# The RWKV scan batches start on the keys alone, and the gate's product moves behind receptances and values

## The chip, the cores and the metric

The kernel runs on one core of a Trainium2 chip. The time is the device time of one execution in microseconds (us). The engines are TensorE (PE in the rows; PEld is its loading of weights), VectorE (DVE), ScalarE (ACT), GpSimd (POOL) and SyncE (SP), which only issues DMA transfers. Every engine works through its own list of instructions, and semaphores tie the lists together.

## The reference, cut to what matters

Two layers act on 256 tokens of width 2048 (128 context tokens, 128 latent ones). The mixer of a layer has three parts side by side, fed by one input projection and merged by one output projection: attention with a sink (12 heads), a Hyena long convolution (512 channels), and the bidirectional RWKV-7 time mixing (768 channels, 12 heads of 64). The change touches the last of these:

```
rkv = short_conv(u_rkv)                      # three taps along the tokens
r, k, v = split(rkv, 3)
decay, a = functions of low-rank products    # w_dn, a_dn
g  = sigmoid(g_dn) @ g_up                    # the gate, low rank 256
kk = k * k_k;  kk = kk / max(norm(kk over a head), 1e-12)
...                                          # the scan, in both directions:
S  = S * decay - (S kk) (kk a) + v k_dir     # one 64x64 state per head
y  = S r
```

The scan of the latent tokens starts from a cached state. Behind the mixer stands an MLP with squared ReLU (hidden width 8192), and every sub-layer sits between two norms with modulation.

## The kernel before, in words

**Products.** The big matrix products run on PE in three passes of reduced fp32 each, so one product is three rows of the profile. `ws` holds the weights still and streams 256 token columns (L508, L511, L512); `as_` holds the activations still and streams up to 512 weight columns (L530, L533, L534). A weight tile comes in by SyncE (`wr`, L231), ScalarE rounds it (`wh`, L232) and VectorE forms the rest (`wl`, L233). Tiles `wr` have four buffers, `wh` and `wl` three each, in a ring: the cast of a tile waits until PE has used the tile three before it. The results of products go to `mm`, of which there are two buffers in PSUM, and each buffer is read by a short convolution (`conv`: one ScalarE instruction L543 and two VectorE instructions L544, L545 for each block of 128 channels) or added up (`acc`). Products `ada` (L387), which make modulation vectors for later, are strewn between the others and also fill gaps.

**Side work.** Everything else that the mixer does is written as generators in a class `Side`: a queue of chains, each of which is stepped on at a rate that depends on the columns of the product just issued (`run`; the rates are the options `sr`, `sq`, `sh`, `so`, `ra`). What a chain yields is a delay before its next step. Their small matmuls stand behind the last product issued, in program order, by a dependency without a semaphore (`beside`); they write to `sm`, with three buffers in PSUM. A scheduler then fixes the order of each engine's list.

**The order in `mixer`.** Low-rank products and the keys k of batch 0, their convolution, the product of the gate and `rwkv_gate`, receptances r and values v of batch 0 (`rkv(0, "rv")`); then the chain of RWKV work joins the side queue. Products of attention's q, k, v follow (512 columns), and attention and Hyena join the queue. Then come k, r, v of batch 1, the three Hyena inputs (256 columns again, the last one feeds tiles `hu0`), and the output projection `w_out` in phases.

**The chain of RWKV work.** It is batch 0 (channel blocks 0 to 2), its output, batch 1 (blocks 3 to 5), its output. A batch (`rwkv_batch`, L1093) waits until r, k and v of its three blocks are there; loads small matrices (`rwkv_up`); loads and transposes the starting states (`rwkv_state`, `rs`); takes the norms of the keys (`rwkv_kk`); runs three scan blocks (`rwkv_stage1`, which goes from the low-rank product L837 through decays and scans on VectorE and ScalarE to the transposes L897, the score products L921 into `sm`, the masked copies L924 and L925, L939 and L942, and the transposes L950); inverts triangular matrices (`rwkv_invert`: reads `rX` by DMA L973, 30 pairs L981 and L982 on VectorE, copies L987 and L988 to `rXo`, writes `rdout` by DMA L994); and finishes (`rwkv_stage2`: reads `rXT` by two DMAs L1002, the products L1021 with `rXT`, L1019 and what follows).

## Time and profile before

| | |
|---|---|
| median of 3 runs | 2888.81 us (2887.84 to 2892.58) |
| the profiled execution | 2894.91 us, span 2893.1 us |
| mean granted clock of TensorE | 0.983 |
| busy: PE / DVE / ACT / POOL | 97% / 57% / 43% / 6% of the span |
| mixer of the first layer | about 160 to 720 us of the span |
| mixer of the second layer | about 1550 to 2125 us of the span |

The page counts an engine as busy while an instruction of its datapath runs. In a timeline row the first number is the start in us from the start of the span, the second the duration, xN the instructions merged into the row, and the brackets at the end give the idle time before it and what ended that. Matmuls overlap in the pipeline, so the distance between starts, not the duration, is what a product costs. PEclk is the granted clock of TensorE as a share of its full speed.

### The profile page before, as it was taken

Reading aid. Unit: us, or ns where it says so; the run is one execution under the profiler, and the core shown is the slowest. Engines: PE = TensorE matmul, PEld = TensorE weight load, DVE = VectorE, ACT = ScalarE, POOL = GpSimd, SP = SyncE. Lnnn points to the kernel's source line nnn. Section 1 sums busy time; section 2 is a strip of 40 time slices with the busy share of each in tenths; the row PEclk is TensorE's granted clock in tenths of the full one; section 3 lists DMA queues with packets and bytes.
Section 4 is the critical chain, followed back from the end, with each engine's and each line's share of the span. In section 5 each row is a group of like instructions: output and inputs, shape, how many; then the busy total and the mean of one; then the engine's idle time right before and its main releaser. Section 6 shows DMA issues by size and latency. Waiting matters only on the chain. (4 is left out here: it accounts for less than half of the span.)

```text
span 2893.1 us, 47892 instructions
## 1 busy us (share of the span) xinstructions
PE 2810.1 (97%) x19163; PEld 2306.6 (80%) x19163; DVE 1646.9 (57%) x2635; ACT 1232.4 (43%) x1878; POOL 179.4 (6%) x368
## 2 busy tenths in 40 slices
PE   6899999999999999999998999999989999999998
PEld 3586888766797897897876979877669989899896
DVE  1356766777544454444455577677675545555555
ACT  2254445434544343343345454453354444444343
POOL 0012101202000000000000111011010000000000
PEclk8999999999999999999999999999899999999999
DMA  9985675478888787887876746534686666666674
GB/s 333 333 300 201 223 231 161 152 261 285 311 268 268 261 270 256 272 274 262 288 279 210 210 149 193 168 111 142 200 297 184 184 186 185 189 189 183 190 241 150
DMA packets 326185, 654.56 MB, mean 226 GB/s; under 512 B 48709, under 2 KB 86158, under 8 KB 325835
## 3 DMA queue, kind: packets, MB, share of 16 engines
q1 hardware_dynamic: 311456, 610.88, 65.3%
q0 software_dynamic: 12928, 36.98, 3.9%
q10 hardware_dynamic: 1579, 3.64, 0.3%
q8 instruction: 150, 2.46, 0.3%
q14 instruction: 72, 0.59, 0.1%
HBM read 632.21 MB, written 19.20 MB: 225 GB/s over the span
## 5 line engine op out<-in xcount | busy, mean ns | idle before, releaser
L233 DVE TENSOR_TENSOR wl<-wr,wh 128x1024 fp32r<-128x1024 f32 (+2 forms) x792 | 929.0, 1175 | 921.1 <-ACT wh L232 909.6
L232 ACT CAST wh<-wr 128x1024 fp32r<-128x1024 f32 (+2 forms) x792 | 798.7, 1010 | 1175.5 <-PE mm L511 522.6
L508 PE MATMUL mm<-acth,wh 128*128 128x256 f32 (+1 forms) x3200 | 921.2, 288 | 6.5 <-ACT acth L489 4.6
L511 PE MATMUL mm<-actl,wh 128*128 128x256 f32 (+1 forms) x3200 | 904.7, 283 | 0.0
L512 PE MATMUL mm<-acth,wl 128*128 128x256 f32 (+1 forms) x3200 | 902.9, 282 | 1.9 <-DVE wl L233 1.9
L508 PEld LDWEIGHTS mm<-acth,wh 128*128 128x128 f32 (+1 forms) x3200 | 601.8, 188 | 59.2 <-issue 32.1
L512 PEld LDWEIGHTS mm<-acth,wl 128*128 128x128 f32 (+1 forms) x3200 | 602.8, 188 | 7.3 <-DVE wl L233 4.3
L511 PEld LDWEIGHTS mm<-actl,wh 128*128 128x128 f32 (+1 forms) x3200 | 600.9, 188 | 4.5 <-issue 3.3
L530 PE MATMUL mm<-wh,fh 128*128 128x512 f32 x1024 | 404.9, 395 | 0.0
L533 PE MATMUL mm<-wl,fh 128*128 128x512 f32 x1024 | 403.3, 394 | 1.0 <-DVE wl L233 0.9
L534 PE MATMUL mm<-wh,fl 128*128 128x512 f32 x1024 | 401.6, 392 | 0.0
L530 PEld LDWEIGHTS mm<-wh,fh 128*128 128x128 f32 x1024 | 192.2, 188 | 56.6 <-issue 8.4
L533 PEld LDWEIGHTS mm<-wl,fh 128*128 128x128 f32 x1024 | 192.2, 188 | 44.9 <-DVE wl L233 2.7
L534 PEld LDWEIGHTS mm<-wh,fl 128*128 128x128 f32 x1024 | 192.0, 187 | 45.2
L387 PE MATMUL ada<-wa,cs 128*32 128x512 f32 x1280 | 193.3, 609 | 8.4 <-DMA wa<-in_ada_w_dram 8.4
L530 PE MATMUL mm<-wh,osh 128*128 128x512 f32 x256 | 106.9, 418 | 0.7 <-ACT osh L1192 0.7
L387 PEld LDWEIGHTS ada<-wa,cs 128*32 128x32 f32 x1280 | 36.6, 109 | 85.9 <-issue 53.6
L533 PE MATMUL mm<-wl,osh 128*128 128x512 f32 x256 | 103.1, 403 | 1.5 <-DVE wl L233 1.5
L534 PE MATMUL mm<-wh,osl 128*128 128x512 f32 x256 | 102.8, 402 | 0.0
L921 PE MATMUL sm<-rZR,rKB 64*128 64x256 f32 x384 | 75.1, 424 | 1.0 <-DVE rLA L925 1.0
L530 PE MATMUL mm<-wh,acth 128*128 128x512 f32 (+1 forms) x192 | 74.3, 387 | 0.0
L533 PE MATMUL mm<-wl,acth 128*128 128x512 f32 (+1 forms) x192 | 68.8, 358 | 0.0
(323 smaller groups left out, 2565.4 us busy)
## 6 DMA issues: line engine op xcount, KB each, us to landing
wr<-in_mlp_w_dram SPq DMA_DIRECT2D x512, 512.0 KB
wa<-in_ada_w_dram SPq DMA_DIRECT2D x352, 512.0 KB
wr<-in_w_in_dram SPq DMA_DIRECT2D x96, 512.0 KB
wr<-in_w_in_dram SPq DMA_DIRECT2D x112, 384.0 KB
wr<-in_w_out_dram SPq DMA_DIRECT2D x56, 512.0 KB
wr<-in_ada_w_dram SPq DMA_DIRECT2D x32, 512.0 KB
gb<-gate POOLq DMA_DIRECT2D x16, 512.0 KB, 8.7
xd<-acc SPq DMA_DIRECT2D x24, 256.0 KB
```

What stands on the lines that cost most here:

```text
L232: nc.scalar.copy(hi, raw)
L233: nc.vector.tensor_sub(lo, raw, hi)
L387: nc.tensor.matmul(ps[32 * j:32 * j + 32, :], lhsT=self.cs[:, kk, :], rhs=w[2 * (kk - k + 1) + j // 2][:, 512 * (j % 2):512 * (j % 2) + 51 ...
L508: m = self.product(nc.tensor.matmul(o, lhsT=h, rhs=hh, start=(k == 0 and b % 2 == 0), stop=False, skip_group_check=True))
L511: nc.tensor.matmul(o, lhsT=h, rhs=hl, start=False, stop=False, skip_group_check=True)
L512: nc.tensor.matmul(o, lhsT=lw, rhs=hh, start=False, stop=(k == KT - 1), skip_group_check=True)
L530: m = self.product(nc.tensor.matmul(o, lhsT=hh, rhs=hi[:, kk, :], start=first, stop=False))
L533: nc.tensor.matmul(o, lhsT=hh, rhs=lo[:, kk, :], start=False, stop=False)
L534: nc.tensor.matmul(o, lhsT=hl, rhs=hi[:, kk, :], start=False, stop=last)
L921: self.beside(nc.tensor.matmul(ps[h][:, i * 256:(i + 1) * 256], lhsT=KB[hs, d, g, i, :], rhs=ZR[hs, d, g, :, :].rearrange("p i t -> p (i t ...
```

## The change

A batch now waits at first for its k alone (with a delay of 1 between looks); then it loads its matrices, loads and transposes the states and takes the key norms; then it waits for r and v (with a delay of 0.25) and goes on as before. In `mixer` the chain joins the side queue behind the convolution of batch 0's k, and `rkv(0, "rv")` comes next; the product of the gate and `rwkv_gate` stand behind it.

```diff
--- before.py
+++ after.py
@@ -1091,12 +1091,15 @@
             yield
 
     def rwkv_batch(self, l, P, bt, u):
-        while any((n, b) not in u for n in "rkv" for b in range(3 * bt, 3 * bt + 3)):
+        waits = lambda names: any((n, b) not in u for n in names for b in range(3 * bt, 3 * bt + 3))
+        while waits("k"):
             yield 1
         self.rwkv_up(l, P, 3 * bt)
         yield from self.rwkv_state(l, P, bt)
         self.R.din = self.dr([2, 12, 128, 128], F32, tag="rdin")
         yield from self.rwkv_kk(P, bt, {b: u["k", b] for b in range(3 * bt, 3 * bt + 3)})
+        while waits("rv"):
+            yield 0.25
         for bi in range(3):
             b = 3 * bt + bi
             if bi < 2:
@@ -1151,12 +1154,11 @@
         self.rwkv_lora(first[0][0], P)
         self.run(first[1][1], 1, ada)
         rkv_conv("k", 0, first[1][0])
+        self.side.add(self.rwkv_batch(l, P, 0, u), self.rwkv_out(l, P, 0), self.rwkv_batch(l, P, 1, u), self.rwkv_out(l, P, 1))
+        rkv(0, "rv")
         ps = self.mm()
         self.run(self.ws(act, W[:, C_G:C_G + 256], [128] * 2, ps), o["sh"], ada)
         self.rwkv_gate(ps, P)
-
-        rkv(0, "rv")
-        self.side.add(self.rwkv_batch(l, P, 0, u), self.rwkv_out(l, P, 0), self.rwkv_batch(l, P, 1, u), self.rwkv_out(l, P, 1))
         qk = [sb([128, 1024], F32, tag="aqk") for g in range(2)]
         v = [sb([128, 256], F32, tag="av") for g in range(2)]
         for c0, n in ((0, 512), (512, 512), (1024, 256)):
```

What this does to the lists of the engines is shown at three places of the second layer. A row gives the line, the instruction, out<-in by the program's names with their numbers, and the form.

The first is TensorE at the head of the first scan block of batch 0, from the transposes L897 on. Before:

```order
L897 MATMUL sm_15980<-const_66,rkf_15964 128x128 x2
L921 MATMUL sm_16011<-rZR_15958,rKB_15959 128x256
L921 MATMUL sm_16012<-rZR_15958,rKB_15959 128x256
L897 MATMUL sm_15980<-const_66,rkf_15978 128x128 x2
L921 MATMUL sm_16011<-rZR_15958,rKB_15959 128x256
L921 MATMUL sm_16012<-rZR_15958,rKB_15959 128x256
L530 MATMUL mm_15765<-wh_15994,acth_14541 128x512
L533 MATMUL mm_15765<-wl_15995,acth_14541 128x512
L534 MATMUL mm_15765<-wh_15994,actl_14542 128x512
L921 MATMUL sm_16027<-rZR_15958,rKB_15959 128x256 x2
L921 MATMUL sm_16028<-rZR_15958,rKB_15959 128x256 x2
L942 MATMUL sm_16041<-rvT_15892,rMA_14669 128x64 x3
```

And in the changed kernel:

```order
L897 MATMUL sm_15778<-const_66,rkf_15750 128x128 x2
L921 MATMUL sm_15803<-rZR_15744,rKB_15745 128x256
L897 MATMUL sm_15778<-const_66,rkf_15770 128x128 x2
L921 MATMUL sm_15804<-rZR_15744,rKB_15745 128x256
L921 MATMUL sm_15803<-rZR_15744,rKB_15745 128x256
L921 MATMUL sm_15804<-rZR_15744,rKB_15745 128x256
L921 MATMUL sm_15819<-rZR_15744,rKB_15745 128x256 x2
L921 MATMUL sm_15820<-rZR_15744,rKB_15745 128x256 x2
L942 MATMUL sm_15845<-rvT_15690,rMA_14669 128x64 x3
L533 MATMUL mm_16005<-wl_16008,acth_14535 128x512
L534 MATMUL mm_16005<-wh_16007,actl_14536 128x512
L921 MATMUL sm_15860<-rZR_15744,rKB_15745 128x256
```

Products L530, L533, L534 stood between the score products L921 after the sixth row; now the first two stand behind the ninth. From L897 to the last L950 of this block there are 21 such rows before and 2 now.

The second is VectorE around the convolution of the last Hyena input (`hu`, from the PSUM buffer `mm_18918` before and `mm_19271` now) and the end of the inversion of batch 1. Before, the convolution stands ahead of the whole inversion:

```order
L233 TENSOR_TENSOR wl_19641<-wr_19639,wh_19640 128x1024
L544 SCALAR_TENSOR_TENSOR hu_2944_19518<-mm_18918,pv_1183_7392,hu_2944_19518 128x2x127
L545 SCALAR_TENSOR_TENSOR hu_2944_19518<-mm_18918,pv_1183_7392,hu_2944_19518 128x2x127
L544 SCALAR_TENSOR_TENSOR hu_2945_19522<-mm_18918,pv_1183_7392,hu_2945_19522 128x2x127
L545 SCALAR_TENSOR_TENSOR hu_2945_19522<-mm_18918,pv_1183_7392,hu_2945_19522 128x2x127
L233 TENSOR_TENSOR wl_19663<-wr_19661,wh_19662 128x1024
L544 SCALAR_TENSOR_TENSOR hu_2946_19526<-mm_18918,pv_1183_7392,hu_2946_19526 128x2x127
L545 SCALAR_TENSOR_TENSOR hu_2946_19526<-mm_18918,pv_1183_7392,hu_2946_19526 128x2x127
```

and behind the copies L987 and L988 come splits of weights:

```order
L981 TENSOR_TENSOR rkt_19899<-rX_19504 112x30
L982 TENSOR_TENSOR rX_19504<-rX_19504,rkt_19899 112x30
L987 COPY rXo_19908<-rX_19504 48x1024
L988 COPY rXo_19908<-rX_19504 48x1024
L233 TENSOR_TENSOR wl_20246<-wr_20244,wh_20245 128x1024
L233 TENSOR_TENSOR wl_20297<-wr_20295,wh_20296 128x1024
L233 TENSOR_TENSOR wl_20351<-wr_20349,wh_20350 128x1024
```

In the changed kernel the convolution stands behind those copies:

```order
L981 TENSOR_TENSOR rkt_19528<-rX_19139 112x58
L982 TENSOR_TENSOR rX_19139<-rX_19139,rkt_19528 112x29x2
L981 TENSOR_TENSOR rkt_19531<-rX_19139 112x30
L982 TENSOR_TENSOR rX_19139<-rX_19139,rkt_19531 112x30
L987 COPY rXo_19546<-rX_19139 48x1024
L988 COPY rXo_19546<-rX_19139 48x1024
L544 SCALAR_TENSOR_TENSOR hu_2975_19629<-mm_19271,pv_1183_7392,hu_2975_19629 128x2x127
L545 SCALAR_TENSOR_TENSOR hu_2975_19629<-mm_19271,pv_1183_7392,hu_2975_19629 128x2x127
L544 SCALAR_TENSOR_TENSOR hu_2976_19633<-mm_19271,pv_1183_7392,hu_2976_19633 128x2x127
L545 SCALAR_TENSOR_TENSOR hu_2976_19633<-mm_19271,pv_1183_7392,hu_2976_19633 128x2x127
L544 SCALAR_TENSOR_TENSOR hu_2977_19637<-mm_19271,pv_1183_7392,hu_2977_19637 128x2x127
L545 SCALAR_TENSOR_TENSOR hu_2977_19637<-mm_19271,pv_1183_7392,hu_2977_19637 128x2x127
```

The eight rows of the convolution moved from ahead of the inversion to behind it.

The third is what feeds and needs that convolution. ScalarE now has its part (L543) behind the cast of `wh_19994`:

```order
L232 CAST wh_19861<-wr_19860 128x1024
L232 CAST wh_19926<-wr_19925 128x1024
L232 CAST wh_19994<-wr_19993 128x1024
L543 ACTIVATE hu_2975_19629<-mm_19271,pv_1183_7392 128x256
L543 ACTIVATE hu_2976_19633<-mm_19271,pv_1183_7392 128x256
L543 ACTIVATE hu_2977_19637<-mm_19271,pv_1183_7392 128x256
L543 ACTIVATE hu_2978_19641<-mm_19271,pv_1183_7392 128x256
L232 CAST wh_20012<-wr_20011 128x1024
```

Before, the casts of ScalarE and the convolution stood like this:

```order
L232 CAST wh_19640<-wr_19639 128x1024
L543 ACTIVATE hu_2944_19518<-mm_18918,pv_1183_7392 128x256
L407 COPY arow_19605<-ada_14733 128x512
L543 ACTIVATE hu_2945_19522<-mm_18918,pv_1183_7392 128x256
L232 CAST wh_19662<-wr_19661 128x1024
L543 ACTIVATE hu_2946_19526<-mm_18918,pv_1183_7392 128x256
L634 COPY hzt_19627<-sm_19585 128x512
L232 CAST wh_19717<-wr_19716 128x512
```

And TensorE starts the next product into the buffer ring, `mm_19859`, behind `mm_19675` (two buffers: it takes that of `mm_19271`):

```order
L530 MATMUL mm_19675<-wh_19844,osh_19671 128x512
L533 MATMUL mm_19675<-wl_19845,osh_19671 128x512
L534 MATMUL mm_19675<-wh_19844,osl_19672 128x512
L387 MATMUL ada_19990<-wa_20244,cs_71 32x512 x2
L387 MATMUL ada_19990<-wa_20421,cs_71 32x512 x2
L387 MATMUL ada_19990<-wa_20485,cs_71 32x512 x2
L387 MATMUL ada_19990<-wa_20557,cs_71 32x512 x2
L387 MATMUL ada_19990<-wa_20610,cs_71 32x512 x2
L387 MATMUL ada_19990<-wa_20696,cs_71 32x512 x2
L387 MATMUL ada_19990<-wa_20784,cs_71 32x512 x2
L387 MATMUL ada_19990<-wa_20851,cs_71 32x512 x2
L530 MATMUL mm_19859<-wh_19861,osh_19651 128x512
```

Of the tiles above, `wh_19844` is the third before `wh_19994` in its ring, and its last reader is the row L534 ahead of the L387 rows; the split of `wh_19994` (`wl_19995`) stands on VectorE 12 rows ahead of the first L544 shown, with nine L981 or L982 rows between it and L987. In the first layer one of the eight rows of that convolution stands ahead of L987 in the changed kernel, and seven behind L988.

Counted over the lists, from the first L837 to the last L950 of a batch: batch 0 has 144 product rows of 512 columns and 42 of 256 between its own, in either layer, and now 102 of 512 and 83 of 256 in the first layer, 102 and 68 in the second. Batch 1 has 252 product rows of 256 columns in the first layer, as before, and 268 instead of 246 in the second; of attention's transposes L742 it has none before and now 24 in each layer. The number of instructions stays the same on TensorE.

## Rows read from the trace of the kernel before

**Rows 1.** Page, part 1: busy time of each engine

```profile
PE 2810.1 (97%) x19163; PEld 2306.6 (80%) x19163; DVE 1646.9 (57%) x2635; ACT 1232.4 (43%) x1878; POOL 179.4 (6%) x368
```

**Rows 2.** Waits of PE, second mixer (1490 to 2160): total, times, longest

```profile
PE sm L897 <- ACT rkf L891: 3.6, 4, 1.8
PE sm L1021 <- DMA rXT<-rdout: 3.1, 2, 1.7
```

**Rows 3.** Windows of the four scan batches: busy us by engine, PEclk, DMA

```profile
221.10:313.30 92.20, 90.30 (x510) 63.36 (x508) 64.17 (x129) 38.91 (x75) 18.35 (x43) 1.00 0.57 193
478.70:567.60 88.90, 85.41 (x569) 68.15 (x568) 68.61 (x147) 38.60 (x82) 16.14 (x39) 0.96 0.40 133
1664.80:1747.40 82.60, 81.35 (x462) 61.62 (x461) 62.35 (x127) 39.51 (x75) 13.69 (x35) 1.00 0.45 140
1902.10:1988.20 86.10, 83.53 (x538) 65.94 (x537) 66.83 (x144) 38.55 (x83) 17.58 (x40) 0.94 0.35 109
```

**Rows 4.** The same windows, PE, line L533 alone

```profile
221.10:313.30 92.20, 23.10 (x63) 1.00 0.57 193
...
1664.80:1747.40 82.60, 23.04 (x63) 1.00 0.45 140
```

**Rows 5.** The same windows, PE, line L511 alone

```profile
478.70:567.60 88.90, 24.20 (x85) 0.96 0.40 133
...
1902.10:1988.20 86.10, 24.21 (x83) 0.94 0.35 109
```

**Rows 6.** Timeline of PE, second layer, around the last scan: start, duration, line

```profile
2044.66 0.40 PE L534 MATMUL mm<-wh,osl 128*128 128x512 f32 x1
...
2050.90 0.40 PE L534 MATMUL mm<-wh,osl 128*128 128x512 f32 x1
2051.23 2.78 PE L387 MATMUL ada<-wa,cs 128*32 128x512 f32 x24
...
2056.59 0.49 PE L1021 MATMUL sm<-rG,rXT 32*32 32x64 f32 x6 [1.41 <-DMA rXT<-rdout]
...
2060.09 2.76 PE L1021 MATMUL sm<-rG,rXT 32*32 32x64 f32 x42 [1.66 <-DMA rXT<-rdout]
```

**Rows 7.** Timeline of PE, 256-column products of the second layer

```profile
1911.80 0.28 PE L508 MATMUL mm<-acth,wh 128*128 128x256 f32 x1
...
1912.51 0.28 PE L508 MATMUL mm<-acth,wh 128*128 128x256 f32 x1
```

**Rows 8.** Windows at half clock: busy us, PEclk

```profile
2059.10:2079.60 20.50, 19.51 (x185) 13.35 (x185) 7.41 (x16) 3.23 (x7) 0.00 (x0) 0.50 0.48 168
2141.00:2144.50 3.50, 3.50 (x10) 0.44 (x12) 3.45 (x6) 3.33 (x11) 0.00 (x0) 0.51 1.04 399
```

**Rows 9.** Timeline of DVE, end of the second layer's last inversion

```profile
2042.26 0.29 DVE L982 TENSOR_TENSOR rX<-rX,rkt 112x130 f32<-112x130 f32 x1
...
2042.78 1.22 DVE L233 TENSOR_TENSOR wl<-wr,wh 128x1024 fp32r<-128x1024 f32 x1
...
2046.00 0.22 DVE L982 TENSOR_TENSOR rX<-rX,rkt 112x30 f32<-112x30 f32 x1
2046.32 0.69 DVE L987 COPY rXo<-rX 48x1024 f32<-48x1024 f32 x1
2047.02 1.15 DVE L988 COPY rXo<-rX 48x1024 f32<-48x1024 f32 x1
```

**Rows 10.** Timeline of ACT, one cast of a weight tile

```profile
2041.61 1.05 ACT L232 CAST wh<-wr 128x1024 fp32r<-128x1024 f32 x1 [1.72 <-PE mm L534]
```

**Rows 11.** Lines of DVE, second mixer: busy, mean ns, idle before

```profile
L544 DVE SCALAR_TENSOR_TENSOR hu<-mm,pv,hu 128x254 f32<-128x254 f32 x12 | 5.7, 476 | 3.0 <-ACT hu L543 3.0
```

**Rows 12.** Timeline of SyncE's queue after that inversion

```profile
2048.47 4.22 SPq L994 DMA_DIRECT2D rdout<-rXo  x8
...
2054.91 0.36 SPq L1002 DMA_DIRECT2D rXT<-rdout  x1
```

**Rows 13.** Lines of PE, second mixer, one line of attention

```profile
L742 PE MATMUL sm<-const,ape 128*128 128x128 f32 x36 | 6.4, 280 | 0.8 <-DVE ape L735 0.8
```

## The prediction

> **What bounds the kernel now.** I read the page first: PE is busy for 97% of the span, VectorE for 57% and ScalarE for 43% [rows 1]. So the time is TensorE's list plus what that list loses, and a change that only reorders can win or lose in four ways: a wait, a stretch at the lower clock, side matmuls that cost more or less because of what stands between them, or a new wait. I read the waits of TensorE next, in the mixers alone. In the second mixer 3.6 us are lost at L897 (four waits on ScalarE's `rkf`) and 3.1 us at L1021, where the products of the last scan wait for `rXT` to come back through memory [rows 2]. Then the windows of the four scan batches with the granted clock: it is 1.00 in both batches 0, which run among 512-column products, and 0.96 and 0.94 in both batches 1, which run among 256-column products [rows 3]. Last the timeline around the end of the second layer's last scan: products that start evenly, 24 matmuls L387, and the two waits of 1.41 and 1.66 us for `rXT` [rows 6]. Right there begins a stretch of 20.5 us at a clock of 0.50, the lower of the two levels, 1.2 instead of 2.4 GHz [rows 8]; a stretch at half speed loses half its length, 10.2 us. The place thus costs 3.1 + 10.2 = 13.3 us.
>
> **The change part by part.** No instruction is added to TensorE; what changes is where the RWKV chain runs. It joins before r and v, so batch 0 starts within the gate's product and each scan comes 25 to 35 us of products earlier. I go through four terms.
>
> **Batch 0, packed closer.** First a price for packing, from the windows. Products of 512 columns start (2050.90 - 2044.66) / 27 = 0.231 us apart, the two rows being first and last of 28 [rows 6]; those of 256 columns 0.71 / 6 = 0.118 us, first and last of seven [rows 7]. L533 is one pass of three. Of its 63 rows in batch 0 [rows 4] 48 stream 512 columns and the rest 256 (144 and 42 rows in three passes by the lists): 144 x 0.231 + 42 x 0.118 = 38.2 us of products in each layer. That leaves 92.2 - 38.2 = 54.0 and 82.6 - 38.2 = 44.4 us for the side matmuls and what they lose [rows 3]. Batch 1 has 85 and 83 rows L511 [rows 5], times three passes and 0.118: 30.1 and 29.4 us. There 88.9 - 30.1 = 58.8 and 86.1 - 29.4 = 56.7 us are left. Hence batches 1 have 8.1 + 8.8 = 16.9 us less of products inside than batches 0, and need 4.8 + 12.3 = 17.1 us more for the same side work: a product pushed out of a batch is paid for in full, because the batch is no shorter without it. Half of that is clock: 0.96 over 88.9 us means 7.1 us at half speed, 3.6 lost, and 0.94 over 86.1 us loses 5.2 [rows 3]. Without these 8.8 us the price is 8.3 / 16.9, about 0.5 us for each us of products pushed out.
>
> By the changed lists batch 0 holds 102 rows of 512 and 83 of 256 in the first layer, 33.4 us, and 102 and 68 in the second, 31.6 us. So 4.8 + 6.6 = 11.4 us are pushed out. At 0.5 that is 5.7, at 1.0 it is 11.4 us. I take 0.7, +8.0 us, since the packed places are more extreme than those of batch 1 (two product rows from L897 to the last L950 of a block). The bounds are 0, if the emptier places simply go by faster, and twice the upper value, 23 us, if a block with nearly nothing inside waits for each masked copy.
>
> On the clock the rows show 1.00 in the sparse batches and 0.94 to 0.96 in the packed ones [rows 3]. The Trainium skill, "TensorE: Matmul & The Clock Gate", section "A second HAM failure mode: psum-queue depth-cycling", says that an engine which idles for moments between groups of matmuls while PSUM buffers are cycled lets the clock swing between its levels, and that this degrades throughput. That speaks against this change, which packs score products through three small buffers. By that rule the price would be the 1.0 with the clock in it, +11.4 us, and the whole sum +0.9 instead of -2.5; by the rows of batch 0 alone, no dips, +5.7.
>
> **Batch 1 beside attention.** Now attention runs inside batch 1. It brings 24 transposes L742 per layer, 0.280 us each [rows 13], so 6.7 us, 13.4 for both layers, and as much VectorE work with them as goes into that. If they fill waits that are now hidden in the packed blocks (86.1 us for 29.4 us of products), all of it is won; if they cost there what they cost elsewhere, nothing. VectorE is busy for 66.8 of these 86.1 us [rows 3], not full, so I take half, -6.7 us. The bounds are -13.4 and, if VectorE's extra work makes the L897 waits twice as long, +3.6 [rows 2]. The second layer's batch 1 also holds 268 product rows instead of 246, 22 x 0.118 = 2.6 us more, by the same price of 0.7 a gain of 1.8 us.
>
> **The end of the second layer.** `rXT` was late because its chain is long: L988 starts at 2047.02 and the second wait ends at 2060.09 [rows 6, 9], with the write at 2048.47 and the second read issued at 2054.91 [rows 12]. That is 13.1 us. In the changed lists L988 itself, 1.15, the convolution, 3.8, and 48 product rows of 0.231, 11.1 us, stand ahead of the first L1021, together 16 us, so `rXT` is in time and the 13.3 us of before go. What is late next stands on VectorE: the convolution of the last Hyena input now stands behind L988, and the next product into the two `mm` buffers, `mm_19859`, needs the one that this convolution reads. From the end of `mm_19675` the chain is: a cast, 1.05 us, which waits for that end because of its ring of three (such a wait for PE stands in [rows 10]); the split, 1.22; nine rows of the inversion of 0.29 down to 0.22 us, about 2.3; the two copies, 0.69 + 1.15 [rows 9]; eight rows of convolution at 0.476 us, 3.8 [rows 11]. That is 10.2 us. TensorE has 16 matmuls L387 for it, at 2.78 / 24 = 0.116 us [rows 6], 1.9 us. So it waits 8.3 us, whatever VectorE did before. Behind the wait the clock will be low for a while. A shorter stretch at 0.51 lasted 3.5 us, 1.7 us lost; the long one cost 10.2 [rows 8]. I take 3, nearer to the short one, since 512-column products follow here and not small ones. New cost 8.3 + 3 = 11.3 against 13.3: -2.0 us, between 8.3 + 1.7 - 13.3 = -3.3 and 8.3 + 10.2 - 13.3 = +5.2, and -13.3 if the wait doesn't form.
>
> All this rests on VectorE not passing over a blocked row; in [rows 9] the starts follow the list. The Trainium skill, "PSUM — Partial Sum Buffer", section "Engine vs sequencer instructions", calls VectorE's and ScalarE's queues strictly first in, first out. By that the term is -2.0 us; if an engine could take the convolution early it would be -13.3 and the sum -13.8.
>
> **The first layer's end, and the rest.** The convolution there is half in front, and TensorE has more products before it needs the buffer; I take 0, with 8.3 us as the worst. What the early steps themselves cost (loading matrices and states on POOL's and SyncE's queues, transposes, key norms) is nothing: they run beside r and v, whose stretch has products alone, and POOL is 6% busy [rows 1]. The gate's product only changes places. If POOL's loads came late, the scan would start where it does now.
>
> **Sum.** 8.0 - 6.7 - 1.8 - 2.0 = -2.5 us, against the profiled execution's 2894.91, so 2892.4. That execution is 6.1 us above the median of 2888.81; I carry the difference over to the median: 2886.
>
> **The rivals.** (a) *Everything fits into gaps.* Attention is won in full, -13.4; packing costs 0.5, +5.7; the second batch gains 1.3; the end -2.0: -11.0 us, 2878. For it: TensorE counts as busy in the batches while small matmuls wait their turn. Against it: VectorE's list gets denser too. (b) *VectorE holds the PSUM buffer in both layers* and the clock stays low behind the wait as long as in [rows 8]. Place: the second product of w_out. Price: 8.3 us in the first layer too, and +5.2 instead of -2.0 in the second: 8.0 - 6.7 - 1.8 + 5.2 + 8.3 = +13.0, 2902. It decides from the point where VectorE reaches L987 of the first layer later than TensorE ends the product before. For it: seven of the eight rows of the convolution stand behind L988 there too. Against it: the split next to them isn't the one that waits for the end of the product. (c) *The wait at `mm_19859` doesn't form*, since TensorE itself comes late: -13.8, 2875. Against it stands the count of 10.2 against 1.9 us. (d) *The change does nothing that counts*: the waits stay where they are, 2889. The moved lists speak against it.
>
> **How the numbers follow.** A measurement of this kernel can tell about 0.2%, 5.8 us, from no change. The forecast has 0.45 (own range 2880 to 2895, three quarters of it within 0.2%), (a) 0.18, (b) 0.24, (c) 0.08, (d) 0.05. Faster by over 0.2%: 0.18 + 0.08 + 0.10 = 0.36. Slower: 0.24 + 0.02 = 0.26. Within: 0.38. The range from 2873 to 2903 takes in (a) to (d) but for their outer halves and the upper bound of packing.
>
> **What would show it.** Packing: batch 0 from its first L837 to its last L950 still 80 us or more in the second layer, with fewer products. Attention: batch 1 not longer than 90 us. End: no wait for `rXT`, one wait of about 8 us at the first row of a w_out product on VectorE's `hu`, and a short stretch at the low clock behind it. I am wrong if batch 0 shrinks by the 6.6 us of products that left it (packing is free), if batch 1 grows by 7 us or more, or if that wait is missing or stands in both layers.

## The result and the profile after

The changed kernel takes 2935.72 us, the median of four runs (2928.7 to 2942.79); the kernel before took 2888.32 beside it (2886.05 to 2892.58). The ratio is 1.0162 [1.013, 1.0195]: 47 us more, where 2886 was forecast with a range up to 2903. The forecast had the sign wrong, and the time lies 33 us above its range.

The profiled execution took 2928.70 us, with a span of 2926.9 and a mean granted clock of 0.979. The first part of its page answers [rows 1]; columns are busy time, share and instructions.

```profile
PE 2825.6 (97%) x19163; PEld 2316.5 (79%) x19163; DVE 1654.1 (57%) x2635; ACT 1229.7 (42%) x1877; POOL 178.8 (6%) x368
```

The list is the same and the busy share too. 97% hides the whole loss, since a side matmul or a product at half the clock counts as busy. So I go on to the waits of TensorE over the whole span. This view's columns are engine and line, what it waited for, us in total, times, longest.

```profile
PE ada L387 <- DMA wa<-in_ada_w_dram: 17.4, 12, 3.8
...
PE sm L897 <- ACT rkf L891: 8.5, 8, 2.0
PE mm L530 <- ACT wh L232: 6.4, 2, 3.6
...
PE sm L831 <- DVE ru_v L545: 1.8, 1, 1.8
...
PE mm L530 <- DVE hu L545: 1.3, 2, 0.6
```

Before, the row of L387 had 8.4 us, and no row had L530 wait for `wh` or `hu`. The waits of L1021 for `rXT` are gone as forecast [rows 2]. In their place stand waits for weights: the modulation weights `wa`, and twice a cast `wh` of a weight of w_out. The windows of the four scan batches answer [rows 3]; the columns are the stretch, its length, busy time and instructions of PE, PEld, DVE, ACT and POOL, the granted clock, the DMA share and GB/s.

```profile
204.80:296.00 91.20, 89.43 (x492) 62.92 (x491) 62.35 (x128) 36.63 (x74) 15.10 (x38) 1.00 0.46 152
444.50:540.40 95.90, 92.95 (x632) 73.27 (x632) 68.82 (x159) 44.07 (x102) 15.05 (x37) 0.98 0.42 143
1659.70:1746.30 86.60, 82.96 (x435) 61.87 (x434) 62.65 (x128) 36.73 (x75) 12.83 (x34) 0.94 0.32 103
1886.00:1977.20 91.20, 89.55 (x606) 73.48 (x604) 70.77 (x163) 45.24 (x105) 15.66 (x38) 1.00 0.31 99
```

Batches 0 last 91.2 and 86.6 us with 5 and 7 us fewer products in them; they lasted 92.2 and 82.6. So a batch did not get shorter by what left it.

To see where the time went I cut both mixers at the same events and took from each stretch its products (0.231 and 0.118 us each) and its L387 matmuls (0.116 each). What is left is what side matmuls, waits and the low clock cost there. Each kernel was profiled twice (the second profiles are experiments 10 and 11 below). The last stretch ends some 96 product rows into the MLP. The table gives the sum of both layers for either profile, and behind the bar the part of it lost at half clock.

```
stretch of a mixer                    before       changed        difference of means (clock)
start to first L837 of batch 0     13.6  13.6 |0 0      19.8  18.7 |1.7 0       +5.7 (+0.9)
batch 0 (first L837, last L950)    88.5  87.3 |0 0     106.1 105.8 |5.1 5.1    +18.1 (+5.1)
between the batches               111.2 111.2 |0 0      88.7  89.7 |0 0        -22.0 (0)
batch 1                           110.1 107.0 |8.5 5.1 119.4 125.5 |1.7 8.5    +13.9 (-1.7)
to the last row of RWKV's output   91.7  85.3 |10.2 3.4 99.7  98.3 |10.2 8.5   +10.5 (+2.6)
rest, into first MLP product       36.2  36.4 |3.4 5.1  52.0  54.3 |13.6 13.6  +16.9 (+9.4)
sum                               451.3 440.8 |22.1 13.6 485.7 492.3 |32.3 35.7 +43.0 (+16.1)
```

The four profiles are 41 us apart in span, (2926.9 + 2932.7 - 2893.1 - 2883.8) / 2. Without the clock each row repeats within 2.3 us from one profile to the other; the clock's part does not. Of the 43 us 27 thus repeat with the lists, and 16 are clock.

The side matmuls of a stretch are the same in both kernels, but for attention's: in each layer 72 of them (L722, L742, L751) stood between the batches, and now 58 stand in batch 1 and 14 behind it (in the first layer 8 small L411 also moved, from batch 1 to the last stretch). So the rows between the batches, of batch 1 and behind it have to be read together.

### The profile page after: what moved, and what is told of

It is laid out like the page before. It is cut to its first block, busy times and chain, and to the rows that moved or that the text cites. A ratio compares the mean times of both kernels' runs of the same rounds, so it can differ in the third digit from the quotient of the medians.

```text
span 2926.9 us, 47902 instructions
## 1 busy us (share of the span) xinstructions
PE 2825.6 (97%) x19163; PEld 2316.5 (79%) x19163; DVE 1654.1 (57%) x2635; ACT 1229.7 (42%) x1877; POOL 178.8 (6%) x368
## 5 line engine op out<-in xcount | busy, mean ns | idle before, releaser
L233 DVE TENSOR_TENSOR wl<-wr,wh 128x1024 fp32r<-128x1024 f32 (+2 forms) x792 | 929.4, 1176 | 942.9 <-ACT wh L232 930.9
L511 PE MATMUL mm<-actl,wh 128*128 128x256 f32 (+1 forms) x3200 | 906.7, 283 | 0.0
L511 PEld LDWEIGHTS mm<-actl,wh 128*128 128x128 f32 (+1 forms) x3200 | 601.6, 188 | 5.5 <-issue 3.7
L530 PE MATMUL mm<-wh,fh 128*128 128x512 f32 x1024 | 405.2, 396 | 0.0
L533 PE MATMUL mm<-wl,fh 128*128 128x512 f32 x1024 | 403.5, 394 | 0.0
L534 PE MATMUL mm<-wh,fl 128*128 128x512 f32 x1024 | 402.0, 393 | 0.0
L530 PEld LDWEIGHTS mm<-wh,fh 128*128 128x128 f32 x1024 | 192.4, 188 | 56.5 <-issue 8.4
L534 PEld LDWEIGHTS mm<-wh,fl 128*128 128x128 f32 x1024 | 192.1, 188 | 45.1
L533 PEld LDWEIGHTS mm<-wl,fh 128*128 128x128 f32 x1024 | 192.4, 188 | 42.8 <-DVE wl L233 0.7
L387 PE MATMUL ada<-wa,cs 128*32 128x512 f32 x1280 | 190.9, 616 | 17.9 <-DMA wa<-in_ada_w_dram 17.4
L530 PE MATMUL mm<-wh,osh 128*128 128x512 f32 x256 | 106.9, 418 | 7.6 <-ACT wh L232 6.4
L387 PEld LDWEIGHTS ada<-wa,cs 128*32 128x32 f32 x1280 | 36.1, 110 | 94.7 <-issue 50.5
L533 PE MATMUL mm<-wl,osh 128*128 128x512 f32 x256 | 105.5, 412 | 2.2 <-DVE wl L233 2.2
L534 PE MATMUL mm<-wh,osl 128*128 128x512 f32 x256 | 104.0, 406 | 0.0
L921 PE MATMUL sm<-rZR,rKB 64*128 64x256 f32 x384 | 83.2, 427 | 0.9 <-DVE rLA L925 0.6
L530 PEld LDWEIGHTS mm<-wh,osh 128*128 128x128 f32 x256 | 49.4, 193 | 28.6 <-ACT wh L232 8.9
L533 PE MATMUL mm<-wl,acth 128*128 128x512 f32 (+1 forms) x192 | 70.5, 367 | 1.0 <-DVE wl L233 1.0
```

The source lines that it names most:

```text
L233: nc.vector.tensor_sub(lo, raw, hi)
L387: nc.tensor.matmul(ps[32 * j:32 * j + 32, :], lhsT=self.cs[:, kk, :], rhs=w[2 * (kk - k + 1) + j // 2][:, 512 * (j % 2):512 * (j % 2) + 51 ...
L511: nc.tensor.matmul(o, lhsT=h, rhs=hl, start=False, stop=False, skip_group_check=True)
L530: m = self.product(nc.tensor.matmul(o, lhsT=hh, rhs=hi[:, kk, :], start=first, stop=False))
L533: nc.tensor.matmul(o, lhsT=hh, rhs=lo[:, kk, :], start=False, stop=False)
L534: nc.tensor.matmul(o, lhsT=hl, rhs=hi[:, kk, :], start=False, stop=last)
```

## The end of the second layer: the wait came, and the loads with it

The timeline of TensorE in the changed kernel at the place that [rows 6] show for before. Columns: start, length, line and operation with its count, and in brackets the idle time ahead with its releaser.

```profile
2033.73 0.40 PE L534 MATMUL mm<-wh,osl 128*128 128x512 f32 x1
2034.06 2.78 PE L387 MATMUL ada<-wa,cs 128*32 128x512 f32 x24
2039.12 1.05 PE L387 MATMUL ada<-wa,cs 128*32 128x512 f32 x4 [2.28 <-DMA wa<-in_ada_w_dram]
2044.00 1.92 PE L387 MATMUL ada<-wa,cs 128*32 128x512 f32 x4 [3.83 <-DMA wa<-in_ada_w_dram]
2046.56 0.76 PE L530 MATMUL mm<-wh,osh 128*128 128x512 f32 x1 [0.63 <-DVE hu L545]
2047.12 0.63 PE L533 MATMUL mm<-wl,osh 128*128 128x512 f32 x1
```

From the end of the row L534 at 2034.13 to 2046.56 are 12.4 us for 32 L387, which are worth 3.7: 8.7 us are lost, where 8.3 were worked out. VectorE in the same stretch, from the end of the inversion, answers [rows 9 and 11]:

```profile
2038.71 0.21 DVE L982 TENSOR_TENSOR rX<-rX,rkt 112x30 f32<-112x30 f32 x1
2039.02 0.69 DVE L987 COPY rXo<-rX 48x1024 f32<-48x1024 f32 x1
2039.72 1.03 DVE L988 COPY rXo<-rX 48x1024 f32<-48x1024 f32 x1
2040.79 0.48 DVE L544 SCALAR_TENSOR_TENSOR hu<-mm,pv,hu 128x254 f32<-128x254 f32 x1
...
2045.41 0.48 DVE L544 SCALAR_TENSOR_TENSOR hu<-mm,pv,hu 128x254 f32<-128x254 f32 x1 [0.54 <-ACT hu L543]
2045.93 0.48 DVE L545 SCALAR_TENSOR_TENSOR hu<-mm,pv,hu 128x254 f32<-128x254 f32 x1
```

The convolution stands behind L988 to the row, and its last one ends at 2046.41, 0.15 ahead of L530. From its first row, at 2040.79, it takes 5.6 us where 3.8 were worked out: three of the four rows L544 wait 0.54 us for ScalarE's L543, and those wait for VectorE's row before them. The row in [rows 11] had that idle time, 3.0 us over twelve rows. But only 0.6 us of the idle time is put down to `hu`; 6.1 us of it are waits of L387 for `wa`. Two chains end within half a microsecond of each other: VectorE's, and that of the loads. In the second profile the row of `hu` is missing, and the loads alone decide. The prediction had 16 L387 there, at a price taken from the trace, and gave them no wait. In the trace the 16 instructions of the list are 32 rows, as the 48 instructions L921 that the code issues in a batch are 96 rows; so they are worth 3.7 us and not 1.9. The last eight wait for two loads, issued at 2035.15 and 2037.06. The window around it shows the clock's part; it answers [rows 8].

```profile
2031.40:2041.60 10.20, 6.49 (x40) 2.70 (x38) 9.74 (x22) 2.47 (x3) 0.34 (x2) 1.00 0.69 207
2041.60:2051.84 10.24, 7.21 (x17) 4.35 (x18) 3.08 (x7) 1.42 (x3) 1.95 (x3) 0.50 0.49 150
```

TensorE had stood idle for 2.28 us and was in the idle time of 3.83 when the clock fell, and 10.24 us at 0.50 cost 5.1, where 3 were taken.

## The tail of the mixers: a place that the prediction left out

In both kernels the last products of w_out are followed by the MLP. Ahead of those stretches POOL issues the loads for the residual (`gb`, `xo`, 4 MB in eight DMAs, `residual_load`). Before, RWKV's output still ran beside the products that came next. In the changed kernel the output of RWKV has ended, and behind its last row 42 us of products of w_out follow in each layer where 16 did (with the 11 us of the MLP up to the cut, 53 and 28). POOL in the changed kernel, second layer:

```profile
2132.62 2.14 POOL L201 DMA_DIRECT2D gb<-gate  x4 [27.83 <-PE mm L530]
2134.93 1.05 POOL L201 DMA_DIRECT2D xo<-xd  x2 [0.17 <-issue]
2136.14 1.05 POOL L201 DMA_DIRECT2D xo<-xd  x2 [0.16 <-issue]
```

The windows behind it, columns as above:

```profile
2130.00:2140.00 10.00, 10.00 (x45) 8.11 (x44) 6.11 (x8) 3.12 (x4) 4.36 (x9) 1.00 0.79 220
2140.00:2150.00 10.00, 10.00 (x56) 6.36 (x55) 6.58 (x12) 4.88 (x10) 2.90 (x6) 1.00 1.03 416
2150.00:2160.00 10.00, 6.49 (x28) 4.72 (x27) 5.41 (x8) 2.90 (x6) 0.99 (x2) 1.00 1.04 342
2160.00:2170.00 10.00, 8.35 (x41) 4.76 (x41) 6.28 (x9) 4.89 (x9) 0.00 (x0) 0.83 0.89 327
```

The DMA share is 1.03 and 1.04: all engines of the core's DMA are taken for 20 us. SyncE issues the weights one by one; between 2125 and 2162 its L231 waits 18.6 us for splits L233, which free a buffer:

```profile
2142.91 0.38 SPq L231 DMA_DIRECT2D wr<-in_w_out_dram  x1
2143.35 0.93 SPq L382 DMA_DIRECT2D wa<-in_ada_w_dram  x2
2147.52 0.33 SPq L231 DMA_DIRECT2D wr<-in_w_out_dram  x1
```

ScalarE's casts of the two `wr`, matched by size (512 and 256 KB) and order, and TensorE:

```profile
2157.49 1.04 ACT L232 CAST wh<-wr 128x1024 fp32r<-128x1024 f32 x1 [6.53 <-DMA wr<-in_w_out_dram]
...
2161.09 0.62 ACT L232 CAST wh<-wr 128x512 fp32r<-128x512 f32 x1 [1.31 <-DMA wr<-in_w_out_dram]
```

```profile
2155.44 0.40 PE L534 MATMUL mm<-wh,osl 128*128 128x512 f32 x1
2158.59 0.50 PE L530 MATMUL mm<-wh,osh 128*128 128x512 f32 x1 [2.75 <-ACT wh L232]
2159.85 0.50 PE L533 MATMUL mm<-wl,osh 128*128 128x512 f32 x1 [0.76 <-DVE wl L233]
```

ScalarE had been waiting 6.53 us for the weight of 512 KB, which was cast 14.6 us after its issue at 2142.91; TensorE had used up what lay ahead and waited 2.75 and 0.76 us. At 2161.0 and 2171.3 follow 3.4 and 17.1 us at half clock. The first layer has the same, with a wait of 3.61. In the changed kernel these loads go out 17 us behind the last row of RWKV's output (2115.2). Before, they began 22 us ahead of it (2117.6) and were issued over 15 us instead of 5, and in a window that was just as full TensorE stood idle nowhere and the clock held:

```profile
2095.76 2.15 POOL L201 DMA_DIRECT2D gb<-gate  x4 [47.32 <-PE mm L530]
```

```profile
2115.00:2125.00 10.00, 10.00 (x49) 7.36 (x48) 6.88 (x14) 4.92 (x12) 0.50 (x1) 1.00 1.02 346
```

## Experiments

The expectations call their theories by letters. A: batch 0 is dear because few products stand in it. D: the tail is dear because of the loads that meet there. G: the wait for `hu` is a cost that can be taken away; against it H, that the same time is lost elsewhere. What else they name is explained in them. Each edit is against the kernel before or the changed one, as said.

### The two halves of the change, each alone

The gate's product behind r and v; the chain joins last, as before:

```diff
+        rkv(0, "rv")
         ps = self.mm()
         self.run(self.ws(act, W[:, C_G:C_G + 256], [128] * 2, ps), o["sh"], ada)
         self.rwkv_gate(ps, P)
-
-        rkv(0, "rv")
         self.side.add(self.rwkv_batch(l, P, 0, u), ...)
```

> The kernel before with one edit: the gate's low-rank product and rwkv_gate stand behind the products of r and v; the RWKV chain joins where it did and a batch waits for r, k and v as it did. The lists give the same products between the scan blocks as before (38.3 us of products in batch 0, 29 to 30 in batch 1). Theory A (the loss of the change comes from scan blocks packed closer): no change, 2888 within 3 us. Theory B (the place of the gate's product costs by itself, by its weights or its tanh): at least 5 us slower, 2893 or more.

2886.82 us, ratio 0.9991 [0.9977, 1.0006]: no change.

The chain joins early and computes norms and states beside r and v; the gate's product stays ahead of them, and the second wait looks less often:

```diff
 against the changed kernel
-            yield 0.25
+            yield 4
...
         self.side.add(self.rwkv_batch(l, P, 0, u), ...)
-        rkv(0, "rv")
         ps = self.mm()
         self.run(self.ws(act, W[:, C_G:C_G + 256], [128] * 2, ps), o["sh"], ada)
         self.rwkv_gate(ps, P)
+        rkv(0, "rv")
```

> The changed kernel with the gate's product put back ahead of r and v, and a delay of 4 instead of 0.25 in the second wait. States and key norms run early, beside the gate, r and v, but the scan blocks start where they start before (96.0 and 1161.6 us of products by the lists) with 36.9 instead of 38.3 us of products in batch 0 and 27.9 and 27.2 instead of 29.8 and 29.1 in batch 1. Theory A (packing): 1.4 to 1.9 us pushed out per batch, near the time of before, 2888 to 2896. Theory B (the early states and norms cost by themselves, in loads or in TensorE's list): most of the loss stays, 2910 or more.

2896.63 us, ratio 1.0019 [1.0004, 1.0034]. The steps moved ahead cost 0.2% where they are, and the gate's place nothing, nearly as the prediction had it. Only together do they start batch 0 some 20 us of products earlier (by the products that lie ahead of it, 55.8 to 35.1 us in the first layer), and only together do they cost 47 us. So the price lies in where the batches and what follows them now run, not in the moved instructions.

### Packing of batch 0

The gate's product gets a lower rate, so that more products stand inside batch 0 of the changed kernel:

```diff
-        self.run(self.ws(act, W[:, C_G:C_G + 256], [128] * 2, ps), o["sh"], ada)
+        self.run(self.ws(act, W[:, C_G:C_G + 256], [128] * 2, ps), 2.5, ada)
```

> The changed kernel with one number changed: during the gate's product the side work is stepped at rate 2.5 instead of 4. Batch 0 starts as early as in the changed kernel (75.2 and 1142.5 us of products), but holds 38.8 and 37.2 us of products, as before (38.3), instead of 33.3 and 31.6. Theory A (packing): the loss of batch 0, 14.4 and 11.0 us in the trace of the changed kernel, mostly goes, 2908 to 2920, the rest being the end of the mixers. Theory C (the early place: side work beside 256-column products, whose weights come in and are split twice as often): the loss stays, 2930 to 2940.

2958.91 us, ratio 1.0241 [1.0219, 1.0263]: far above what was expected. Batch 0 has as many products as before again (39.1 and 37.4 us), and loses 52.6 and 47.2 us where the changed kernel lost 52.1 and 54.0 in the first profile: better in the second layer, not in the first. So the total speaks against theory A, and so does batch 0, which should have won most of its loss back; C had it that the loss stays, but C's 2930 to 2940 was missed too. The new loss lies elsewhere: over both layers and against the first profile of the changed kernel, 20.5 us more between the batches, 8.2 in batch 1 and 8.9 in the tails, and L387 waits 29.3 us for `wa`.

The opposite in the kernel before: a higher rate beside attention's products, so that batch 0 has fewer of them (21.7 and 26.9 instead of 38.6 us).

```diff
-            ... sq=3, ...
+            ... sq=6, ...
```

> The kernel before with one number changed: the side work beside attention's q, k, v is stepped at rate 6 instead of 3. The scan blocks of batch 0 start where they did (93.3 and 1158.9 us of products) among 512-column products, but hold 21.5 and 26.5 us of products instead of 38.3, so 16.8 and 11.8 us are pushed out, and everything behind runs 27 us of products earlier, as in the changed kernel. Theory A (packing): at least as slow as the changed kernel, 2925 to 2950. Theory C (the early place beside 256-column products): nothing of this kind here, at most the end of the mixers (about 5 to 15 us), 2893 to 2905.

2985.22 us, ratio 1.0328 [1.0299, 1.0356], above the 2950 that theory A allowed. The windows of both batches 0:

```profile
219.60:305.30 85.70, 82.65 (x384) 56.48 (x383) 58.08 (x121) 32.57 (x68) 15.88 (x38) 0.88 0.38 127
1700.70:1791.60 90.90, 86.28 (x380) 61.35 (x379) 60.59 (x123) 34.97 (x72) 13.67 (x33) 0.86 0.28 89
```

With 28.6 us fewer products both together are 1.8 us longer than before, 176.6 against 174.8 [rows 3]. The loss rises by 35.0 us, 23.1 of them at the half clock that these rows show as 0.88 and 0.86, which neither batch 0 had before. The other 11.9 are no more than the 13.0 that the changed kernel loses without the clock, with 17 us more products inside. What pays most is one line, the score products that are written into the small PSUM buffers. The groups by line of the second layer's batch 0 (columns: tiles, shapes and count, busy us, mean ns of one, idle time) in the kernel before, in experiment 3, in the second profile of the changed kernel and in experiment 4:

```profile
L921 PE MATMUL sm<-rZR,rKB 64*128 64x256 f32 x96 | 15.9, 404 | 0.0
```

```profile
L921 PE MATMUL sm<-rZR,rKB 64*128 64x256 f32 x96 | 18.4, 406 | 0.3 <-DVE rLA L925 0.3
```

```profile
L921 PE MATMUL sm<-rZR,rKB 64*128 64x256 f32 x96 | 20.7, 411 | 0.0
```

```profile
L921 PE MATMUL sm<-rZR,rKB 64*128 64x256 f32 x96 | 27.4, 503 | 0.0
```

The same 96 matmuls keep TensorE busy for 15.9, 18.4, 20.7 and 27.4 us with 38.6, 37.4, 31.9 and 26.9 us of products among them (the last at a clock of 0.86). One of them takes 404 to 411 ns in the first three; what grows is the distance from one to the next, 158 to 208 ns from the first to the third row by their starts. From start to next start the line takes 30.9 us in both batches 0 of the kernel before, and 39.3 in the two of the changed kernel that have no dip, one in each profile: 8.4 of the 13.0 us. In experiment 3 it takes 35.0, so half of that came back.

The other direction in the kernel before, a lower rate beside attention's products (42.1 us of products in each batch 0):

```diff
-            ... sq=3, ...
+            ... sq=2.7, ...
```

> The kernel before with one number changed: the side work beside attention's q, k, v is stepped at rate 2.7 instead of 3, so batch 0 holds 41.8 us of products in both layers instead of 38.3 and what follows runs about 4 us of products later. Theory A (packing; from the runs so far 0.6 to 1.7 us for each us of products pushed out of batch 0): 4 to 8 us faster, 2881 to 2885. Rival F (a block costs nothing more once it holds as much as before, and the later end of the chain costs): 2888 to 2895.

2926.83 us, ratio 1.0124 [1.0103, 1.0145]; theory A had 2881 to 2885, rival F 2888 to 2895. Batch 0 gains nothing, as F has it: 43.3 and 45.1 lost, together 88.4 against 88.5, where A had 4 to 8 us less. But batch 1 comes later and falls into half clock:

```profile
491.90:599.90 108.00, 102.47 (x552) 73.82 (x551) 72.28 (x152) 39.95 (x85) 16.27 (x40) 0.83 0.36 119
```

This one window loses 18.8 us at the clock, the second layer's 11.9. A theory of batch 0 alone does not forecast the time of such a kernel.

### The loads of the tail

The residual's loads one phase of w_out earlier, in the changed kernel:

```diff
-            if ph == 2:
+            if ph == 1:
                 self.residual_load(P, 2)
```

> The changed kernel with the loads of gate vectors and residual for the end of the mixer (4 MB on POOL's queue, residual_load) issued ahead of the second phase of w_out instead of the third; the scan blocks stay as they are. Theory D (the end of the mixers: the RWKV chain is gone by then, 53 us of bare products with their weights meet these 4 MB and the weights of the modulation, and TensorE waits for weights and drops to the low clock): the waits of L530 on wh (3.6 and 2.8 us in the changed kernel's trace) go and the loss of the last stretch, 41.9 and 33.5 us before the MLPs, falls by 12 to 18 us in all, 2918 to 2926 against 2936. Rival E (the last stretch only shows the bare products that side work covered elsewhere, loads don't matter): 2932 to 2940.

2919.9 us (2913.97 to 2927.88), ratio 1.0092 [1.0069, 1.0115]: 15.8 us less than the changed kernel's median. The windows of its tail, at the times shown above:

```profile
2140.00:2150.00 10.00, 10.00 (x45) 8.10 (x44) 5.66 (x7) 3.00 (x4) 2.57 (x6) 1.00 0.84 295
2150.00:2160.00 10.00, 10.00 (x45) 8.11 (x44) 8.94 (x14) 6.20 (x12) 1.39 (x3) 1.00 0.57 177
2160.00:2170.00 10.00, 9.07 (x52) 5.49 (x50) 9.73 (x15) 6.87 (x15) 0.00 (x0) 1.00 0.76 248
```

The DMA is not full, TensorE does not wait for `wh`, and the clock is 1.00. The tails lose 21.4 and 19.9 us instead of 25.9 and 26.1, 10.7 us less. (The profile is of the slowest of this kernel's four runs and loses 6.7 us more than the first profile of the changed kernel at half clock in batches 0, so its span of 2926.1 hides the gain.)

Earlier loads in the kernel before, as a control. They go out with the last column group of phase 1, 15 us earlier in the second layer (2081.19), where experiment 5 moved them by a whole phase, 19 us (2113.91):

```diff
+                if ph == 1 and cg == 3:
+                    self.residual_load(P, 2)
...
-            if ph == 2:
-                self.residual_load(P, 2)
```

> Control: the kernel before with the same loads issued ahead of the last quarter of the second phase of w_out instead of ahead of the third phase. Theory D: the last stretch has room there, as the RWKV output still runs beside the products; no change, 2886 to 2892. If the loads cost wherever they stand at the end, 4 us or more is won, below 2884.

2890.56 us, ratio 1.0000 [0.9985, 1.0016]. Where RWKV's output covers the loads, this shift changes nothing. So of the 16.9 us that the tails lose more, 11 to 12 (against the first profile and against the mean of both) come from loads that meet bare products, shown by taking it away and by the control; experiment 7 below, with the same early loads, has the same 41 us in its tails. Some 5 us stay. What the time won beyond the tails, 4 to 5 us, is not assigned.

Both repairs at once, the early loads and a fuller batch 0:

```diff
-            ... sq=3, ...
+            ... sq=2.6, ...
...
-            if ph == 2:
+            if ph == 1:
```

> The run with the loads issued earlier, and besides the side work beside q, k, v stepped at rate 2.6 instead of 3: batch 0 holds 37.5 and 35.8 us of products instead of 33.3 and 31.6. Theory A and D together: 4.2 us more inside at 0.6 and 1.7 each, 10 us, beyond what the loads win, 2906 to 2918. If packing isn't what batch 0 pays for: the same as the run with the loads alone.

2942.93 us, ratio 1.0188 [1.0161, 1.0214]: 23 us worse than the early loads alone, against the expectation. Batch 0 loses 105.1 instead of 111.8 us; without the clock 91.5 instead of 100.0, 8.5 us for 8.3 us of products put back, as theory A says. The first layer's batch 1 loses 79.5 instead of 60.6, 17.1 of it at half clock, and 11.9 more are lost at half clock ahead of it. It is experiment 6 over again.

All profiles side by side, us of both batches 0 together, cut as in the table above:

```
kernel                     products   loss without   clock
                           inside     the clock
experiment 6                  84          88.4         0
before (twice), 1, 8          77       87.3 to 88.5    0
experiment 3                  77          98.3         1.5
experiment 2                  74          91.9         0
experiment 7                  74          91.5        13.6
changed (twice)               65       100.7, 101.0    5.1, 5.1
experiments 5, 9              65       100.0, 100.1   11.8, 10.2
experiment 4                  49          100.4       23.1
```

Between 77 and 65 us of products the loss grows by about as much as leaves; above and below that it stays. Experiment 3 doesn't fit, so how many products stand inside isn't all of it, and where they stand was not varied alone. Dips fall into batches 0 in every kernel whose batches 0 start early, and in experiment 4; in none of the six other profiles.

### The convolution ahead of the scan's end

Early loads, and a longer delay ahead of the inversion, so that the last Hyena convolution is issued first and L530 need not wait for `hu`:

```diff
-            ... w0=1, ...
+            ... w0=3, ...
...
-            if ph == 2:
+            if ph == 1:
```

> The run with the loads issued earlier, and besides a delay of 3 instead of 1 ahead of each inversion. By the lists this puts the convolution of the last Hyena input ahead of the copies L987 and L988 in both layers; batch 0 is as it was, batch 1 starts 4 us of products later. Theory G (the convolution behind the inversion holds a product buffer for 8 to 9 us in the second layer, and the low clock follows): the stretch from the end of batch 1's scan blocks to its output in the second layer loses 8 to 13 us less (53.4 us without the modulation products in the run before), 2906 to 2914 against 2919.9. Rival H (rXT is late in its place again, as in the kernel before, because less stands between): that stretch loses the same, 2915 to 2925.

2927.84 us, ratio 1.0138 [1.0102, 1.0174]: no gain over the early loads alone, 8 us worse by the medians, and above what either theory had. In the second layer the wait for `hu` is gone, and so are the waits for `wa` at that place. But the stretch to RWKV's last row loses 55.9 us, with early loads alone 53.4. L387 waits 17.1 us for `wa` in all, as with the change (17.4; with early loads alone 20.4), and a wait as long as the one that went shows up 80 us later:

```profile
2120.12 1.06 PE L387 MATMUL ada<-wa,cs 128*32 128x512 f32 x6
2124.93 1.92 PE L387 MATMUL ada<-wa,cs 128*32 128x512 f32 x2 [3.75 <-DMA wa<-in_ada_w_dram]
```

So the wait at `mm_19859` was not VectorE's alone, and theory G fails. H was right that the time is lost elsewhere, but not in its reason: no wait for `rXT` came back.

### Both kernels profiled again

No edit. The question is which of the half-clock stretches belong to the lists.

> The changed kernel itself, unaltered, profiled once more. Of its 34 us more of span the first profile showed 7 us more lost at the lower clock than before. Theory L (the dips belong to the lists): the dips stand again in the second layer's batch 0 (5.1 us lost in the first profile, 8.5, 8.5 and 6.8 in three kernels with the same lists there), behind the wait for hu in the second layer and in both tails, and the span is 2925 to 2945. Theory H (chance of a run): they stand elsewhere, and batch 0 of the second layer loses nothing at the clock.

> The kernel before, unaltered, profiled once more. The prediction credited 13.3 us at the end of the second layer, 10.2 of them a stretch at the lower clock; two kernels with the same lists at that place lost 3.4 there. Theory L: 10.2 us are lost there again. Theory H (chance of a run): 0 to 5, and the span is below 2893.

2934.46 and 2885.55 us. The batches of the changed kernel, second layer, then of the kernel before:

```profile
1662.10:1744.60 82.50, 79.39 (x435) 59.15 (x434) 62.41 (x128) 36.66 (x74) 12.82 (x34) 1.00 0.35 107
1884.30:1983.20 98.90, 97.16 (x606) 79.40 (x606) 71.16 (x163) 45.43 (x105) 15.62 (x38) 0.91 0.29 91
```

```profile
1662.70:1744.90 82.20, 81.25 (x462) 61.60 (x461) 61.93 (x127) 39.38 (x75) 13.68 (x35) 1.00 0.44 142
1899.70:1985.70 86.00, 83.41 (x538) 66.43 (x537) 66.84 (x144) 38.42 (x83) 17.47 (x40) 0.94 0.34 109
```

In the batches chance decides where a dip falls: in the changed kernel the second layer's batch 0 went from 0.94 to 1.00 and its batch 1 from 1.00 to 0.91, and the first layer's batch 0 from 1.00 to 0.95. Each of the changed kernel's two profiles has 5.1 us of dips in batches 0, before's none. In the tails (13.6 us in both) and at the end of the second layer (10.2 and 8.5) they come back: there theory L is right. And in the kernel before the 20.5 us stretch of [rows 8] lasted 6.8 this time. The 10.2 us that the prediction credited were worth 3.4.

## Why the prediction was wrong

**The rest of the mixer: taken as nothing, measured +16.9 in the tails.** This is the step that failed most. The prediction followed the scans and stopped at the end of RWKV; it asked what would be late next on VectorE, but not what would run, once RWKV ended earlier, beside the products left behind. There 4 MB of residual loads, the modulation weights and the products' own weights share the DMA, with nothing on TensorE to cover them. Of the 16.9 us 9.4 are clock. Moving the loads took 11 to 12 us out of the tails, and did nothing in the kernel before.

**Batch 0, packed closer: +8.0, measured +18.1.** The direction was right: batches got no shorter by the 11.7 us of products that left them (11.4 by the count). The size was wrong. The list's own part is 13.0 us, a price of 1.1 for each us pushed out where 0.7 was chosen; and 5.1 of clock stand on top, which the rows of before, 1.00 in both batches 0, did not show. The bounds of 0 to 23 held it; the choice between them leaned on batch 1. That comparison left the L387 in: batches 0 hold 80 rows of them and batches 1 48, 3.7 us, so the price without the clock was (17.1 + 3.7 - 8.8) / 16.9 = 0.7 and not 0.5, and with it 1.2. The Trainium skill, "TensorE: Matmul & The Clock Gate", section "A second HAM failure mode: psum-queue depth-cycling", has TensorE idle for moments and its clock swing where PSUM buffers are cycled; the measured 5.1 us agree in direction, and no run shows that this was the reason. That emptiness alone makes the price is not shown either. Experiment 7 bears it out (1.0 for each us put back); experiment 3 does not, nor do 4 and 6, outside 65 to 77 us of products.

**Beside attention: -6.7 and -1.8, measured -8.1, by luck.** The stretch between the batches lost 22.0 us less and batch 1 took 13.9 of that back. But the term's reason fails. It took 0.280 us for a transpose L742, which is its length and not the distance to the next start. Before, second layer, four of them and the product behind:

```profile
1783.60 0.60 PE L742 MATMUL sm<-const,ape 128*128 128x128 f32 x4
1783.96 0.36 PE L508 MATMUL mm<-acth,wh 128*128 128x256 f32 x1
```

That is 0.09 us each. By starts all 36 between the batches take 4.0 and 3.4 us, so the 24 that moved were worth 2.3 to 2.7 us in a layer and not 6.7; in batch 1 they take 2.8 and 3.6. All of attention's rows (L722, L742, L751) take 17.8 us less between the batches, 18.0 more in batch 1 of the first profile, and 1.8 more behind it. Their move won nothing. The 8.1 us come from other rows of both stretches, and why is open. Batch 1 alone grew by 7.0 and 5.1 us in the first profiles, to 95.9 and 91.2; the prediction named 7 us or more as a sign against it.

**The end of the second layer: -2.0, measured +9.3** (from 48.3 and 41.9 to 55.1 and 53.7, batch 1's end to the last row of RWKV's output). `rXT` was in time, and TensorE lost 8.7 us at `mm_19859` (8.3 worked out). That these agree is luck: VectorE's chain took 12.4 us and not 10.2, and the L387 3.7 and not 1.9. Apart from the clock the stretch lost 6.7 more, against 8.3 - 3.1 = 5.2 by the prediction; about 0.9 of it are 14 rows L751 that moved here. What failed is the credit: 10.2 us of [rows 8] were taken as the price of the waits for `rXT`, from one profile. A second one shows 3.4, while the changed kernel loses 8.5 to 10.2, in the first profile 5.1 of it in a dip ahead of the place (at 2000.6). So the clock gave +2.6 where the prediction had 3 - 10.2 = -7.2. And the wait was put on VectorE alone: only 0.6 us of it is put down to `hu`, and the loads of `wa` were as late.

**The first layer's end: 0, measured +1.2. The early steps: 0, measured +5.7.** The wait for `hu` in the first layer was 0.6 us, not the 8.3 of rival (b). Of the 5.7, ahead of batch 0, TensorE's waits for `ru_v` (1.8) and for a sine of the Hyena filter at L588 (2.1), both in the first layer, are 3.9; neither was there before. Experiment 2 has the early steps without them.

**The rivals.** None of them named the tail. (b) at 2902 had the right side with the wrong place; (a) and (c) had the wrong side, and (d) no change.

What stays open: what makes half-clock stretches fall into batch 1 when its list hardly changes (experiments 6 and 7, 18.8 and 17.1 us in one window), why experiment 3 lost 24 us more than the changed kernel, and what else than emptiness batch 0 pays for. The sum of the table, 43 us, is short of the 47 by the medians; the profiles carry 41. No version run here was faster than the kernel before by more than the noise.

## What to carry to other kernels

When a change makes a chain of side work end earlier, look at the far end: list what ran beside the products there, and which loads were covered by it, before the near end is costed at all. A stretch at half clock that stands in one profile is no credit to be spent; take a second profile of the same kernel and spend only what stands in both. Where side matmuls depend on each other, products among them can be nearly free, but only up to a point: here those between 65 and 77 us were, those above were not. Price a small matmul by the distance between starts, and count rows of the list and rows of the trace in one unit before they meet in a sum.

## What the runs showed of the hardware

- The same program loses 22.1 and 13.6 us at half clock in its two mixers in two executions, and the stretch behind the same wait lasted 20.5 and 6.8 us. The rest of the loss repeated within 2.3 us per stretch.
- With a full DMA (share 1.02 to 1.04) TensorE had no idle time in a window where side matmuls stood among the products; where products stood alone it waited 2.75 and 3.61 us for a weight, and taking the extra loads away there took 11 to 12 us out of both tails. A weight of 512 KB was cast 14.6 us after its issue there.
- Ninety-six score products kept TensorE busy between 15.9 and 20.7 us at full clock, with 38.6 to 31.9 us of products among them, at the same 404 to 411 ns each.
